# Two transformer blocks with split fp32 weights: the convolution with tokens on partitions, kr's first half from x without norm, two load queues and products of ones at first, and side jobs spread by traced durations

## The chip, the cores and the metric
One core of a Trainium2 chip. The metric is the device time of one execution in microseconds (us); one execution was profiled, and its trace is read here.

## The reference, cut to what matters
Two blocks run one after the other on 256 tokens of width 2048, batch 1, all fp32. Cut to what the change touches:

```
h = rms_norm(x) * norm_gain                    # block 1; u = h @ w_in, split into
q, k, v, z_a, f | r, kr, vr, z_b, w, a | g_a, g_b   # fox attention, rwkv7, two gates
u_rwkv = u + (u shifted by one token - u) * mu      # token shift of r, kr, vr, z_b, w, a
...
h = rms_norm(x) * norm_g_2                     # block 2; proj = h @ w_in_2, split into
cg, cb, cu, cz, c_q, c_kv, k_rope, mla_z, mem_q, mem_z, g_conv, g_mla, g_mem
conv_y = cb * causal_depthwise_conv(cg * cu, w)     # 3 taps along the tokens, 1024 channels
o_conv = (conv_y * silu(cz)) @ w_conv_out
o_mla, o_mem = latent attention of 16 heads, attention to 256 memory tokens
x = x + (sigmoid(g_conv)*o_conv + sigmoid(g_mla)*o_mla + sigmoid(g_mem)*o_mem) @ w_o
```

## The kernel before, in words
**Weights.** All weights lie in HBM as 659 blocks of 128x1024 fp32 (512 KB). SP loads a block into `raw` (`dma_to`, line 396), ACT rounds it to fp32r as `whi` (line 279), DVE subtracts the two as `wlo` (line 242). Four `raw` and four `whi`/`wlo` buffers exist. Activations are split in the same manner into a high and a low part. Each product of an activation with a weight is then three matmuls on PE: high by high, high by low, low by high, all from line 287.

**Two forms of gemm** (`gemm`, line 472). In the plain form the weights are the stationary operand, 256 columns (the tokens) stream, and each of four accumulators holds 128 channels by 256 tokens. In the form marked `tm` the activations are stationary, 512 weight columns stream, and each of two accumulators holds 128 tokens by 512 channels. There are five accumulator banks (`gpool`) and three banks for all else (`ppool`). The gates `ga`, `gb`, `gm`, `gc`, `gl`, the output projections and some others are `tm`; the convolution's four projections `cg`, `cu`, `cb`, `cz` are plain, twice each (`conv_groups(b)`, line 1494, for 512 channels at a time). After the last matmul of an accumulator, `evac` reads it on ACT or DVE; until then its bank is not free.

**The convolution before.** Channels are on partitions and tokens in the free direction, so a tap is a multiply by a column of parameters (`cw0` to `cw2`) with the source shifted by one or two columns. `cz` is gated and split at once into the pair `och`, `ocl`, which the gemm `co` takes later.

**Side jobs.** The recurrence of rwkv7, the attentions and the norms are generators (`spawn`). `pump()` (line 459), called between the matmuls of a gemm, steps them as long as an estimate of DVE's and ACT's time (`clock`) isn't too far ahead of an estimate of PE's. The costs in the estimate are constants: `CD` a DVE instruction, `CA` an ACT instruction, and a term in `mm` for a matmul. `finish(job)` steps a job to its end at once. A scheduler then fixes each engine's order from the order in which this recording wrote it; every engine runs its list in order, so an instruction that waits holds all that stands behind it. `hr` (in `head_rs`, line 597) is a per-head reciprocal root: DVE computes `hy` on a compact tile, a DMA of POOL writes it to HBM (`hd`), and two DMAs of POOL read it back in broadcast form.

**The start.** x comes in four tiles `xt`. Each is squared (ACT), reduced on DVE (`red`, to `r4`) and, after the last tile, summed over partitions by a product with ones, `ssq`; in the program's order the four `ssq` stand between the first gemms. Those gemms (the small `lora` ones and `r`) run from x times gain without the norm (`xg`), and the factor `rs` is applied at evacuation (`evac_scaled`, line 704); `kr` and `vr` follow from `h`, which `start_job` (line 752) makes. `par` (parameters) and `xt` are loaded by SP, interleaved with the first weights (lines 325, 388 to 396).

Of the kernel before, what the change touches and what calls it, by code (L numbers as in the profile page):

```python
# [26 lines left out]
def weight_groups():  # L27
# [4 lines left out]
    g = []  # L32
# [32 lines left out]
    def conv(b):  # L65
        for i, nm in enumerate(("cg", "cu", "cb", "cz")):
            add(f"{nm}{b}", w, 2048, _tiles((0, 2048, 1024, 3072)[i] + 512 * b, 4))

# [44 lines left out]
def pack_weights(inputs):  # L113
# [20 lines left out]
    ("fbias", 1), ("w0", 8), ("a0", 8), ("k_k", 8), ("k_a", 8), ("r_k", 8), ("ln_w", 8), ("ln_b", 8),  # L134
    ("fng", 16), ("ng2", 16), ("cw0", 8), ("cw1", 8), ("cw2", 8), ("qg", 4), ("kvg", 4),
    ("qn_g", 1), ("qr_g", 1), ("kn_g", 1), ("kr_g", 1), ("mem_g", 16), ("mqn_g", 2), ("mkn_g", 2),
# [9 lines left out]
def pack_params(inp):  # L146
    def flat(n):
        return np.asarray(inp[n]).reshape(-1)

    mix = flat("rwkv_shift_mix")  # L150
    zeros = np.zeros(128, np.float32)

    def padded(v):
        return np.concatenate([v, zeros[:128 - len(v)]])

    fb = np.zeros(128, np.float32)
    fb[96:104] = flat("fox_forget_bias")
    cw = np.asarray(inp["conv_w_2"]).reshape(3, 1024)
    v = {
        "norm_gain": flat("norm_gain"), "mu_r": mix[0:1024], "mu_kr": mix[1024:2048], "mu_vr": mix[2048:3072],  # L160
        "mu_zb": mix[3072:4096], "mu_wd": padded(mix[4096:4192]), "mu_ad": padded(mix[4192:4288]), "fbias": fb,
        "w0": flat("rwkv_w0"), "a0": flat("rwkv_a0"), "k_k": flat("rwkv_k_k"), "k_a": flat("rwkv_k_a"),
        "r_k": flat("rwkv_r_k"), "ln_w": flat("rwkv_ln_w"), "ln_b": flat("rwkv_ln_b"),
        "fng": flat("final_norm_gain"), "ng2": flat("norm_g_2"), "cw0": cw[0], "cw1": cw[1], "cw2": cw[2],
        "qg": flat("mla_q_norm_g_2"), "kvg": flat("mla_kv_norm_g_2"), "qn_g": flat("mla_qn_nope_g_2"),
        "qr_g": np.tile(flat("mla_qn_rope_g_2"), 2), "kn_g": flat("mla_kn_nope_g_2"),
        "kr_g": np.tile(flat("mla_kn_rope_g_2"), 2), "mem_g": flat("mem_norm_g_2"),
        "mqn_g": flat("mem_qn_g_2"), "mkn_g": flat("mem_kn_g_2"),
    }
# [58 lines left out]
def hybrid_kernel(ctx: ExitStack, tc: tile.TileContext, io, out):  # L228
# [95 lines left out]
    xt = [a4("xt") for _ in range(4)]  # L324
    nc.sync.dma_start(out=par, in_=io["params"])

# [53 lines left out]
    def dma_to(n):  # L380
        while st["dma"] < min(n, nblk):
            i = st["dma"]
            j = block_at(i)
            raw_t[j] = wpool.tile([128, 1024], F32, name=nm("raw"), tag="raw", bufs=NRAW)
            x = i // 3
            if i == 0:
                for p in range(2):
                    nc.sync.dma_start(out=xt[0][:, 2 * p:2 * p + 2, :], in_=io["xT"][:, 2 * p:2 * p + 2, :])
                    nc.sync.dma_start(out=raw_t[j][:, half(p)], in_=io["W"][j, :, half(p)])
            else:  # L390
                if i % 3 == 0 and x < 4:
# [239 lines left out]

    def sumsq_start(tiles, scales=None):

        ps = bank("ssq")
        n = len(tiles)
        for i, x in enumerate(tiles):
            sq = a4("sq")
            act(sq, x, AF.Square)
            r = b1("sqr")
            red(r, sq.rearrange("p a t -> p t a"), ALU.add)  # L640
            yield
            mm(ps[:, :256], ones, r, start=i == 0, stop=i == n - 1)
        sumsq_start.out = ps[:, :256]
# [772 lines left out]
    def latent_job(d, gain, name):  # L1416
# [74 lines left out]
    oc = []  # L1491
    cg = {}

    def conv_groups(b):
        gemm(f"cg{b}", h2, evac_copy(cg, b, "cg"))
        g, cv = cg.pop(b), out4("cv")

        def evac_u(c, ps):
            k = 4 * b + c
            u, v = g[:, c, :], cv[:, c, :]  # L1500
            mul(u, u, ps)
            ts(v, u, pc("cw2", k), ALU.mult)
            stt(v[:, 1:256], u[:, 0:255], pc("cw1", k), v[:, 1:256], ALU.mult, ALU.add)
            stt(v[:, 2:256], u[:, 0:254], pc("cw0", k), v[:, 2:256], ALU.mult, ALU.add)
        gemm(f"cu{b}", h2, evac_u)
        gemm(f"cb{b}", h2, lambda c, ps: mul(cv[:, c, :], cv[:, c, :], ps))
# [3 lines left out]
        def evac_cz(c, ps):  # L1510
            t = b1("cz")
            silu2(t, ps)
            stt(t, t, 0.5, cv[:, c, :], ALU.mult, ALU.mult)
            split(t, p[0][:, c, :], p[1][:, c, :])
# [258 lines left out]
```

## Time and profile before

| | |
|---|---|
| median of 3 runs | 2058.05 us (2056.01, 2058.05, 2065.45) |
| the profiled execution: its own time, its span | 2055.2 us, 2053.4 us |
| PE busy | 2021.0 us, 98% |
| DVE, ACT, POOL busy | 1304.9 us (64%), 968.3 us (47%), 73.9 us (4%) |
| HBM read | 365.76 MB, 181 GB/s over the span |

The profile's page gives busy times by engine, the chain of work that ended last (followed back from the last instruction), and the costliest groups. A matmul's record is longer than the distance to the next one, since they overlap; its price is therefore the distance between two starts. The granted clock is given for a stretch as a share of TensorE's full speed: 1.00 is 2.4 GHz, 0.50 is 1.2 GHz.

### The profile page before, as it was taken

To read this page: it belongs to the slowest core of one execution; us is meant where nothing else is said; L and a number is where in the kernel's file an instruction comes from. 1 tells how busy PE (TensorE), PEld (TensorE's weight loads), DVE (VectorE), ACT (ScalarE), POOL (GpSimd) and SP (SyncE) were. 2 spreads that over 40 slices of the span, in tenths; PEclk is the share of its full clock that TensorE was granted. 3 is DMA by queue.
4 is the path that set the end of the run, shared out by engine and by line. 5 is a ranking of instruction groups with operands and counts; after the bars stand their busy time and mean duration, and the time that the engine had idled before them with its cause. 6 is when DMAs were issued, how large, how long until landed. Compare 5 with 4: busy or idle time off the path is not lost.

```text
span 2053.4 us, 33342 instructions
## 1 busy us (share of the span) xinstructions
PE 2021.0 (98%) x13456; PEld 1822.4 (89%) x13456; DVE 1304.9 (64%) x1987; ACT 968.3 (47%) x1334; POOL 73.9 (4%) x133
## 2 busy tenths in 40 slices
PE   8999999998998999999999999999999999999999
PEld 8999989897777888898999999998888889988887
DVE  8776737868446478666865776755755655555554
ACT  6634435444444445554554435445545444444442
POOL 0002000020000000000000000000000000000000
PEclk9999999999999999999999999999999999999999
DMA  7555644544546656665555554556655555566564
GB/s 248 172 182 166 199 131 135 175 134 156 171 155 217 213 191 211 194 209 185 193 188 182 157 175 154 196 164 193 207 185 176 193 172 179 195 212 201 192 195 154
DMA packets 105674, 374.97 MB, mean 183 GB/s; under 512 B 12920, under 2 KB 13904, under 8 KB 105520
## 3 DMA queue, kind: packets, MB, share of 16 engines
q1 hardware_dynamic: 97568, 350.73, 52.8%
q0 software_dynamic: 7952, 22.12, 3.7%
q8 instruction: 105, 1.72, 0.3%
q14 instruction: 49, 0.40, 0.1%
HBM read 365.76 MB, written 5.86 MB: 181 GB/s over the span
## 4 chain that ended last, share of the span: by engine, by line
PE 94%; DMA 2%; DVE 2%; issue 1%; ACT 1%; POOL 0%; SPq 0%; DVEq 0%; ACTq 0%; POOLq 0%
PE acc.lz L287 4%; PE acc.ga L287 4%; PE acc.gb L287 4%; PE acc.gl L287 4%; PE acc.wo L287 4%; PE acc.w L287 4%; PE acc.lo L287 4%; PE acc.gc L287 4%; PE acc.gm L287 4%; PE acc.fq L287 2%; PE acc.r L287 2%; PE acc.zb L287 2%; PE acc.mz L287 2%; PE acc.mq L287 2%; PE acc.fk L287 2%; PE acc.mk L287 2%
## 5 line engine op out<-in xcount | busy, mean ns | idle before, releaser
L242 DVE TENSOR_TENSOR wlo<-raw,whi 128x1024 fp32r<-128x1024 f32 (+1 forms) x659 | 795.7, 1221 | 540.1 <-ACT whi L279 529.9
L279 ACT ACTIVATE whi<-raw 128x1024 fp32r<-128x1024 f32 (+1 forms) x659 | 683.1, 1055 | 757.3 <-issue 88.1
L287 PE MATMUL acc.lz<-h2h,whi 128*128 128x256 f32 x256 | 72.6, 284 | 0.0
L287 PE MATMUL acc.lz<-h2l,whi 128*128 128x256 f32 x256 | 72.6, 284 | 0.0
L287 PE MATMUL acc.lz<-h2h,wlo 128*128 128x256 f32 x256 | 72.5, 283 | 0.0
L287 PE MATMUL acc.gb<-wlo,hh 128*128 128x512 f32 x128 | 50.5, 398 | 6.0 <-DVE wlo L242 6.0
L287 PE MATMUL acc.ga<-whi,hh 128*128 128x512 f32 x128 | 50.9, 402 | 4.5 <-DVE zb L262 4.5
L287 PE MATMUL acc.ga<-whi,hl 128*128 128x512 f32 x128 | 51.2, 400 | 0.0
L287 PE MATMUL acc.ga<-wlo,hh 128*128 128x512 f32 x128 | 50.8, 397 | 0.0
L287 PE MATMUL acc.gb<-whi,hl 128*128 128x512 f32 x128 | 50.3, 397 | 0.0
L287 PE MATMUL acc.gl<-whi,h2h 128*128 128x512 f32 x128 | 50.0, 392 | 0.0
L287 PE MATMUL acc.gl<-wlo,h2h 128*128 128x512 f32 x128 | 50.0, 392 | 0.0
L287 PE MATMUL acc.gc<-whi,h2l 128*128 128x512 f32 x128 | 50.0, 392 | 0.0
L287 PE MATMUL acc.gl<-whi,h2l 128*128 128x512 f32 x128 | 50.0, 392 | 0.0
L287 PE MATMUL acc.w<-wlo,mgh 128*128 128x512 f32 x128 | 50.0, 390 | 0.0
L287 PE MATMUL acc.w<-whi,mgl 128*128 128x512 f32 x128 | 49.9, 390 | 0.0
L287 PE MATMUL acc.gm<-wlo,h2h 128*128 128x512 f32 x128 | 49.9, 391 | 0.0
L287 PE MATMUL acc.gc<-wlo,h2h 128*128 128x512 f32 x128 | 49.9, 391 | 0.0
L287 PE MATMUL acc.gm<-whi,h2l 128*128 128x512 f32 x128 | 49.8, 390 | 0.0
L287 PE MATMUL acc.gb<-whi,hh 128*128 128x512 f32 x128 | 49.6, 397 | 0.0
L287 PE MATMUL acc.wo<-whi,ml 128*128 128x512 f32 x128 | 49.5, 390 | 0.0
L287 PE MATMUL acc.wo<-wlo,mh 128*128 128x512 f32 x128 | 49.5, 389 | 0.0
(627 smaller groups left out, 6192.6 us busy)
## 6 DMA issues: line engine op xcount, KB each, us to landing
raw<-in_W SPq DMA_DIRECT2D x657, 512.0 KB, 4.0
hr<-hd POOLq DMA_DIRECT2D x10, 512.0 KB, 5.6
hr<-hd POOLq DMA_DIRECT2D x12, 256.0 KB, 5.5
xr<-in_xtm POOLq DMA_DIRECT2D x4, 512.0 KB, 6.6
mt<-in_memT POOLq DMA_DIRECT2D x4, 512.0 KB, 6.5
xbd<-x1g POOLq DMA_DIRECT2D x4, 512.0 KB, 3.0
xo<-xbd POOLq DMA_DIRECT2D x4, 512.0 KB, 5.3
out_tm<-xo SPq DMA_DIRECT2D x8, 256.0 KB, 4.2
```

Of the source, the lines that this page charges most:

```text
L242: DVE.tensor_tensor(out=o, in0=a, in1=b, op=op)
L279: ACT.activation(out=o, in_=a, func=f, scale=scale, **kw)
L287: TE.matmul(o, lhsT=l, rhs=r, start=start, stop=stop)
```

## The change
1. The convolution's four projections become `tm` (512 weight columns stream over stationary activations). Tokens are then on partitions, so a tap is no longer a shift of columns: `conv_job` copies u = cg*cu by DMAs of POOL to `ul`, one and two tokens (partitions) later, loads the taps broadcast to all partitions (`cw`, a new input `cwt`), and DVE multiplies and adds 512 columns at a time. `evac_cb` finishes that job before it reads cb's accumulator. The result is turned to channels on partitions by 16 transposes on PE (`make_pair`) before it is split.
2. At the start: `par` and the first x tile are issued by ACT's queue, the weights by SP's; five products of ones (`NWARM`) go to `ssq` before any data; the partial sums of squares are folded by adds on DVE (`fold`) and summed by one product of ones instead of four. The memory tokens' sum of squares and the two latent norms are folded likewise.
3. `kr`'s first half runs from `xg` with `rs` applied at evacuation; `start_job` is finished behind it, not ahead.
4. The constants of the estimates: `CD` 0.065 to 0.15, a matmul's cost 0.0133 + n/2400 us for n columns (at least 0.109), fp32 products n/600.

```diff
-            add(f"{nm}{b}", w, 2048, _tiles((0, 2048, 1024, 3072)[i] + 512 * b, 4))
+            add(f"{nm}{b}", w, 2048, _tiles((0, 2048, 1024, 3072)[i] + 512 * b, 4), tm=True)
...
-        clock["pe"] += max(0.000424 * n, 0.0001 + 0.0016 * fsz(l) / 2) if l.dtype == F32R else max(0.00168 * n, 0.00168 * fsz(l))
+        clock["pe"] += max(PEF + n / 2400.0, 0.109) if l.dtype == F32R else max(n / 600.0, fsz(l) / 1200.0)
...
-    nc.sync.dma_start(out=par, in_=io["params"])
+    nc.scalar.dma_start(out=par, in_=io["params"])
...
+    ssq = bank("ssq")[:, :256]
+    for _ in range(NWARM):
+        TE.matmul(ssq, lhsT=ones, rhs=one1.to_broadcast([128, 256]), start=True, stop=True)
...
-                    nc.sync.dma_start(out=xt[0][:, 2 * p:2 * p + 2, :], in_=io["xT"][:, 2 * p:2 * p + 2, :])
+                    nc.scalar.dma_start(out=xt[0][:, 2 * p:2 * p + 2, :], in_=io["xT"][:, 2 * p:2 * p + 2, :])
...
+    def fold(sq, r, i):
+
+        add(sq[:, 0:2, :], sq[:, 0:2, :], sq[:, 2:4, :])
+        if i:
+            add(r, r, sq[:, 0, :])
+            add(r, r, sq[:, 1, :])
+        else:
+            add(r, sq[:, 0, :], sq[:, 1, :])
...
-        red(r4[:, i, :], sq.rearrange("p a t -> p t a"), ALU.add)
+        fold(sq, r0, i)
...
-            for i in range(4):
-                mm(ssq, ones, r4[:, i, :], start=i == 0, stop=i == 3)
+            mm(ssq, ones, r0)
...
-    finish(j0)
-    xg.clear()
...
-    for key in ("kr", "vr"):
-        gemm(f"{key}0", h, evac_shift(key, 0))
+    gemm("kr0", xg, evac_scaled("kr", 0))
+    finish(j0)
+    xg.clear()
+    gemm("vr0", h, evac_shift("vr", 0))
...
+    def conv_job(b, u):
+
+
+        w = [tm4(a4("cw")) for _ in range(2)]
+        late = [tm4(a4("ul")) for _ in range(2)]
+        for i in range(2):
+            n = i + 1
+            POOL.memset(late[i][0:n, 0, :], 0.0)
+            POOL.dma_start(out=late[i][n:128, :, :], in_=u[0:128 - n, :, :])
+            POOL.dma_start(out=late[i][0:n, 1, :], in_=u[128 - n:128, 0, :])
+        POOL.dma_start(out=w[0], in_=io["cwt"][:, b, 0:2, :])
+        POOL.dma_start(out=w[1][:, 0, :], in_=io["cwt"][:, b, 2, :])
+        yield from lag()
+        wb = [w[1][:, 0, :], w[0][:, 1, :], w[0][:, 0, :]]
+        for t in range(2):
+            mul(u[:, t, :], u[:, t, :], wb[0])
+            yield
+            for i in range(2):
+                mul(late[i][:, t, :], late[i][:, t, :], wb[1 + i])
+                add(u[:, t, :], u[:, t, :], late[i][:, t, :])
+                yield
...
-        gemm(f"cg{b}", h2, evac_copy(cg, b, "cg"))
...
+        g = tm4(out4("cg"))
+        gemm(f"cg{b}", h2, lambda t, ps: acopy(g[:, t, :], ps))
+        gemm(f"cu{b}", h2, lambda t, ps: mul(g[:, t, :], g[:, t, :], ps))
+        jc = spawn(conv_job(b, g))
+
+        def evac_cb(t, ps):
+            finish(jc)
+            mul(g[:, t, :], g[:, t, :], ps)
+        gemm(f"cb{b}", h2, evac_cb)
...
+        def evac_cz(t, ps):
+            x = b2("cz")
+            act(x, ps, AF.Tanh, scale=0.5)
+            stt(x, x, 1.0, ps, ALU.add, ALU.mult)
+            stt(g[:, t, :], x, 0.5, g[:, t, :], ALU.mult, ALU.mult)
         gemm(f"cz{b}", h2, evac_cz)
+        make_pair(b, g, p)
...
+NWARM = 5
...
-CD, CA = 0.065, 0.17
+CD, CA, PEF = 0.15, 0.17, 0.0133
```

The new constants move instructions of the side jobs on DVE. Two places, both around a wait of PE. The first is where the second half of the recurrence's bonus (`CE`, `BV`) waits for its broadcast `hr`, between the last step of `hy`, from which that broadcast is made, and `CE`. DVE's list before:

```order
655 L242 TENSOR_TENSOR hy_6521<-hy_6521,ht_6522 128x256
656 L559 MEMSET mf_6581 128x1
657 L262 SCALAR_TENSOR_TENSOR mf_6581<-gate_6367,acc.pf_997_6596 128x512
658 L559 MEMSET gate_6665 128x1
659 L262 SCALAR_TENSOR_TENSOR mf_6581<-gate_6367,acc.pf_996_6595 128x512
660 L559 MEMSET mf_6815 128x1
661 L559 MEMSET gate_6893 128x1
662 L242 TENSOR_TENSOR obl_6916<-BV_1812,obh_6915 128x1024
663 L262 SCALAR_TENSOR_TENSOR mf_6815<-gate_6665,acc.pf_1038_6829 128x512
664 L262 SCALAR_TENSOR_TENSOR CE_6411<-CE_6411,par,hr_6537 128x256 x4
665 L262 SCALAR_TENSOR_TENSOR BV_4562<-CE_6411,par,BV_4562 128x256 x2
```

And DVE's list now:

```order
682 L241 TENSOR_TENSOR hy_6692<-hy_6692,ht_6693 128x256
683 L241 TENSOR_TENSOR wlo_7037<-raw_6966,whi_7036 128x1024
684 L561 MEMSET mf_6830 128x1
685 L261 SCALAR_TENSOR_TENSOR mf_6830<-gate_6638,acc.pf_1040_6845 128x512
686 L561 MEMSET gate_6908 128x1
687 L241 TENSOR_TENSOR wlo_7043<-raw_6972,whi_7042 128x1024
688 L261 SCALAR_TENSOR_TENSOR mf_6830<-gate_6638,acc.pf_1039_6844 128x512
689 L241 TENSOR_TENSOR obl_6931<-BV_1827,obh_6930 128x1024
690 L241 TENSOR_TENSOR wlo_7077<-raw_7004,whi_7076 128x1024
691 L261 SCALAR_TENSOR_TENSOR CE_6576<-CE_6576,par,hr_6738 128x256 x4
```

Three blocks of `wlo` stand between `hy` and `CE` where none stood.

The second is the evacuation of the first accumulator of `zb`'s second half, with the steps of the triangular solve (`TM`, `W`) ahead of it. The solve's steps widen from 64x31 to 64x256 and narrow again. DVE's list before (the steps at 64x220 and at 64x231 to 64x252 stand ahead of these rows):

```order
528 L242 TENSOR_TENSOR TM_5425<-W_752_5183,W_751_5182 64x255
529 L242 TENSOR_TENSOR W_752_5183<-W_752_5183,TM_5425 64x17x15
530 L242 TENSOR_TENSOR TM_5440<-W_752_5183,W_751_5182 64x256
531 L242 TENSOR_TENSOR W_752_5183<-W_752_5183,TM_5440 64x16x16
532 L242 TENSOR_TENSOR TM_5443<-W_752_5183,W_751_5182 64x255
533 L242 TENSOR_TENSOR W_752_5183<-W_752_5183,TM_5443 64x15x17
534 L262 SCALAR_TENSOR_TENSOR zb_5470<-acc.zb_762_5207,par,zb_5470 128x255
```

And DVE's list now (ahead of these rows another `wlo` and the steps up to the first at 64x135):

```order
525 L241 TENSOR_TENSOR wlo_5574<-raw_5370,whi_5573 128x1024
526 L241 TENSOR_TENSOR W_776_5350<-W_776_5350,TM_5429 64x27x5
527 L241 TENSOR_TENSOR TM_5432<-W_776_5350,W_775_5349 64x156
528 L241 TENSOR_TENSOR W_776_5350<-W_776_5350,TM_5432 64x26x6
529 L241 TENSOR_TENSOR TM_5447<-W_776_5350,W_775_5349 64x175
530 L241 TENSOR_TENSOR W_776_5350<-W_776_5350,TM_5447 64x25x7
531 L241 TENSOR_TENSOR TM_5450<-W_776_5350,W_775_5349 64x192
532 L561 MEMSET mf_6092 128x1
533 L241 TENSOR_TENSOR W_776_5350<-W_776_5350,TM_5450 64x24x8
534 L241 TENSOR_TENSOR TM_5453<-W_776_5350,W_775_5349 64x207
535 L241 TENSOR_TENSOR W_776_5350<-W_776_5350,TM_5453 64x23x9
536 L261 SCALAR_TENSOR_TENSOR zb_5480<-acc.zb_750_5154,par,zb_5480 128x255
```

The evacuation now stands after the steps up to 64x207, with two `wlo` among them (one is in these rows, the other just ahead); before, it stood after those up to 64x256 and the first past it.

## Rows read from the trace of the kernel before

**Rows 1.** The profile's page: busy time, share of the span and instructions by engine; then the chain that ended last, by engine.

```profile
PE 2021.0 (98%) x13456; PEld 1822.4 (89%) x13456; DVE 1304.9 (64%) x1987; ACT 968.3 (47%) x1334; POOL 73.9 (4%) x133
...
PE 94%; DMA 2%; DVE 2%; issue 1%; ACT 1%; POOL 0%; SPq 0%; DVEq 0%; ACTq 0%; POOLq 0%
```

**Rows 2.** What PE waited for: engine, waiting tile and line, the releaser, us in total, times, longest us.

```profile
PE lora L287 <- ACT xgh L279: 6.2, 1, 6.2
PE acc.gb L287 <- DVE wlo L242: 6.0, 1, 6.0
PE acc.ga L287 <- DVE zb L262: 4.5, 1, 4.5
PE acc.fz L287 <- DVE wlo L242: 2.3, 1, 2.3
...
PE ms L287 <- DVE mq L262: 1.2, 1, 1.2
PE mpt L1632 <- DVE msm L256: 1.0, 1, 1.0
```

**Rows 3.** The chain in order of time: start us, us, engine, tile, line, number of instructions. `cz` streams 256 columns, `lo` 512.

```profile
1213.35 17.04 PE acc.cz L287 x142
...
1805.71 21.76 PE acc.lo L287 x96
```

**Rows 4.** Timeline of PE, start us and us: six transposes in a row.

```profile
875.02 0.82 PE L530 MATMUL tr<-con,hx 128*128 128x128 f32 x6
```

**Rows 5.** Windows: us, busy of PE, PEld, DVE, ACT, POOL (with counts), the granted clock (PEclk), DMA share, GB/s. Rows of two such tables.

```profile
635.40:640.00 4.60, 4.59 (x11) 3.63 (x12) 4.60 (x9) 0.00 (x0) 0.56 (x1) 0.50 0.71 231
480.50:482.00 1.50, 1.49 (x4) 1.20 (x5) 0.85 (x2) 0.95 (x3) 0.00 (x0) 0.50 0.00 0
...
6.00:13.00 7.00, 6.81 (x27) 6.12 (x28) 6.72 (x9) 5.79 (x10) 0.00 (x0) 1.00 1.00 373
13.00:20.00 7.00, 7.00 (x59) 6.95 (x58) 6.92 (x12) 7.00 (x12) 0.00 (x0) 1.00 1.05 382
```

**Rows 6.** Timeline of DVE around the wait for `hr` at 632 us: start us, us, instruction, and in brackets the idle time before it and its releaser.

```profile
626.48 0.68 DVE L262 SCALAR_TENSOR_TENSOR mf<-gate,acc.pf 128x512 f32<-128x512 f32 x1
631.76 1.67 DVE L262 SCALAR_TENSOR_TENSOR CE<-CE,par,hr 128x256 f32<-128x256 f32 x4 [4.59 <-DMA hr<-hd]
...
634.14 1.22 DVE L242 TENSOR_TENSOR wlo<-raw,whi 128x1024 fp32r<-128x1024 f32 x1
```

**Rows 7.** Timeline of PE right behind that wait.

```profile
635.41 0.79 PE L287 MATMUL acc.gb<-wlo,hh 128*128 128x512 f32 x1 [5.98 <-DVE wlo L242]
...
636.42 0.63 PE L287 MATMUL acc.gb<-whi,hh 128*128 128x512 f32 x1
636.85 0.63 PE L287 MATMUL acc.gb<-wlo,hh 128*128 128x512 f32 x1
...
640.69 0.41 PE L287 MATMUL acc.gb<-wlo,hh 128*128 128x512 f32 x1
```

**Rows 8.** Timeline of DVE ahead of the evacuation of `zb`.

```profile
457.79 0.18 DVE L242 TENSOR_TENSOR TM<-W,W 64x31 f32<-64x31 f32 x1
...
479.65 0.42 DVE L242 TENSOR_TENSOR W<-W,TM 64x255 f32<-64x255 f32 x1
479.99 0.47 DVE L262 SCALAR_TENSOR_TENSOR zb<-acc.zb,par,zb 128x255 f32<-128x255 f32 x1
```

**Rows 9.** Timeline of PE in the first 20 us.

```profile
8.15 0.41 PE L287 MATMUL lora<-xgh,whi 128*128 128x256 f32 x1
8.36 0.41 PE L287 MATMUL lora<-xgl,whi 128*128 128x256 f32 x1
...
10.34 1.22 PE L287 MATMUL ssq<-sqr,one 128*128 128x256 f32 x2
...
11.57 0.41 PE L287 MATMUL acc.r<-xgl,whi 128*128 128x256 f32 x1
...
12.78 0.28 PE L287 MATMUL acc.r<-xgl,whi 128*128 128x256 f32 x1
12.90 0.28 PE L287 MATMUL lora<-xgh,wlo 128*128 128x256 f32 x1
...
19.12 0.59 PE L287 MATMUL ssq<-sqr,one 128*128 128x256 f32 x2
...
19.67 0.28 PE L287 MATMUL lora<-xgh,whi 128*128 128x256 f32 x1
```

**Rows 10.** Timeline of the start on DVE, SP's queue and ACT.

```profile
0.81 0.06 DVE L342 MEMSET one<- 128x1 f32 x1 [0.81 <-PEq L1765]
...
1.65 0.42 SPq L389 DMA_DIRECT2D raw<-in_W  x1
...
5.10 0.63 ACT L279 ACTIVATE whi<-raw 128x512 fp32r<-128x512 f32 x1 [3.09 <-DMA raw<-in_W]
```

**Rows 11.** Groups of DVE's instructions by line and form: line, engine, operation, tiles, shapes, number | busy us, mean ns of one | idle before it. The second and third rows are of the stretch 1190 to 1290 us.

```profile
L270 DVE TENSOR_REDUCE sqr<-sq 128x256 f32<-128x1024 f32 x8 | 16.1, 2031 | 0.3 <-ACT sq L279 0.3
...
L242 DVE TENSOR_TENSOR cv<-cv,acc.cb 128x256 f32<-128x256 f32 x4 | 1.7, 415 | 0.0
...
L242 DVE TENSOR_TENSOR oml<-mof,omh 128x512 fp32r<-128x512 f32 x2 | 1.4, 686 | 0.0
```

**Rows 12.** The page's DMA issues: tiles, queue, number, KB each, median us from issue to landing.

```profile
hr<-hd POOLq DMA_DIRECT2D x10, 512.0 KB, 5.6
```

More of the change, by code (lines that the diff above doesn't have):

```diff
@@ L134 @@
     ("fbias", 1), ("w0", 8), ("a0", 8), ("k_k", 8), ("k_a", 8), ("r_k", 8), ("ln_w", 8), ("ln_b", 8),
-    ("fng", 16), ("ng2", 16), ("cw0", 8), ("cw1", 8), ("cw2", 8), ("qg", 4), ("kvg", 4),
+    ("fng", 16), ("ng2", 16), ("qg", 4), ("kvg", 4),
     ("qn_g", 1), ("qr_g", 1), ("kn_g", 1), ("kr_g", 1), ("mem_g", 16), ("mqn_g", 2), ("mkn_g", 2),
@@ L157, in pack_params @@
     fb[96:104] = flat("fox_forget_bias")
-    cw = np.asarray(inp["conv_w_2"]).reshape(3, 1024)
     v = {
@@ L163, in pack_params @@
         "r_k": flat("rwkv_r_k"), "ln_w": flat("rwkv_ln_w"), "ln_b": flat("rwkv_ln_b"),
-        "fng": flat("final_norm_gain"), "ng2": flat("norm_g_2"), "cw0": cw[0], "cw1": cw[1], "cw2": cw[2],
+        "fng": flat("final_norm_gain"), "ng2": flat("norm_g_2"),
         "qg": flat("mla_q_norm_g_2"), "kvg": flat("mla_kv_norm_g_2"), "qn_g": flat("mla_qn_nope_g_2"),
@@ L630, in hybrid_kernel, with sumsq_start @@
     dma_to(NRAW)
-    def sumsq_start(tiles, scales=None):
+    def fold(sq, r, i):
[5 more added lines that the diff above has]
+            add(r, sq[:, 0, :], sq[:, 1, :])
+    def sumsq_start(tiles):
         ps = bank("ssq")
-        n = len(tiles)
+        r = b1("sqr")
         for i, x in enumerate(tiles):
@@ L638, in sumsq_start @@
             act(sq, x, AF.Square)
-            r = b1("sqr")
-            red(r, sq.rearrange("p a t -> p t a"), ALU.add)
+            fold(sq, r, i)
             yield
-            mm(ps[:, :256], ones, r, start=i == 0, stop=i == n - 1)
+        mm(ps[:, :256], ones, r)
         sumsq_start.out = ps[:, :256]
@@ L663, in hybrid_kernel @@
     xg = []
-    r4 = a4("sqr")
+    r0 = b1("sqr")
     def start_tile(i):
@@ L711, in evac_scaled @@
         return f
-    ssq = bank("ssq")[:, :256]
     acc_l = [bank("lora")[:, :256] for _ in range(2)]
@@ L749, in hybrid_kernel @@
                 del hi_t[j], lo_t[j]
-    del ssq, r4
+    del ssq, r0
     def start_job():
@@ L1421, in latent_job @@
         r = b1("lr")
-        red(r, sq.rearrange("p a t -> p t a"), ALU.add)
+        fold(sq, r, 0)
         yield
@@ L1491, in hybrid_kernel @@
     oc = []
-    cg = {}
-    def conv_groups(b):
-        gemm(f"cg{b}", h2, evac_copy(cg, b, "cg"))
[L1496 to L1506, printed above, removed]
+    def conv_job(b, u):
[17 more added lines that the diff above has]
+                yield
+    def conv_groups(b):
+        g = tm4(out4("cg"))
[6 more added lines that the diff above has]
+        gemm(f"cb{b}", h2, evac_cb)
         p = out_pair("oc")
         oc.append(p)
[L1510 to L1514, printed above, removed]
+        def evac_cz(t, ps):
[3 more added lines that the diff above has]
+            stt(g[:, t, :], x, 0.5, g[:, t, :], ALU.mult, ALU.mult)
         gemm(f"cz{b}", h2, evac_cz)
+        make_pair(b, g, p)
     lo = {}
@@ L1755 @@
         "fng": np.ascontiguousarray(np.broadcast_to(a["final_norm_gain"].reshape(1, 2048), (128, 2048))),
+        "cwt": np.ascontiguousarray(np.broadcast_to(
+            a["conv_w_2"].reshape(3, 2, 512).transpose(1, 0, 2)[None], (128, 2, 3, 512))),
         "memT": channel_major(a["mem_2"]),
```

## The prediction
> **What bounds the kernel now.** Read the page first: PE is busy 98% of the span, and the chain that ended last is PE for 94% of it [rows 1]. So the time is what PE issues, priced by the distance between two starts, plus the few places where PE stands still. The list of what PE waited for names those: 6.2 us for the first data, 6.0 us at `acc.gb`, 4.5 us at `acc.ga`, 2.3 us at `acc.fz`, about 1 us each at `ms` and `mpt` [rows 2]. DVE at 64% and ACT at 47% matter only where their list in order makes one of these waits, and DMA only at the start. The sum is made against the profiled execution, 2055.2 us; it lies 2.9 us below the median of the three runs. Half a per cent, some 10 us, is about what a measurement of this kernel can tell from no change.
>
> **Wider streams in the convolution.** The eight gemms issue 1536 matmuls of 256 columns and would issue 768 of 512. A run of `cz` takes 17.04/142 = 0.120 us a matmul, a run of `lo`, which has the new form, 21.76/96 = 0.2267 us [rows 3]. 768 x (0.240 - 0.2267) = **-10.2 us**, all of it on PE and so on the path. The new form loads a stationary tile for each matmul as `lo` does, so nothing is left to find out here.
>
> **Transposes.** 16 more on PE. Six in a row take 0.82 us with a record of 0.27 each [rows 4], so (0.82 - 0.27)/5 = 0.11 us from one to the next: **+1.8 us**. The bounds are 0 (they fill a gap) and the whole record, 16 x 0.27 = 4.3. I take the spacing, because here too they come in fours between matmuls. The Trainium skill, TensorE: Matmul & The Clock Gate, section "Part 4: PE-mode transpose", speaks against this part: it gives about 275 ns for a transpose in a kernel. This trace's record agrees with that length but not with that price, as the next one starts 0.11 us later; by the page's figure the term would be 4.4 us and the forecast 2.6 us higher, an estimate.
>
> **The wait at `gb`.** DVE's list reaches `CE` after `mf` at 626.48, idles 4.59 us for the broadcast `hr`, and only behind `CE` and `BV` makes the next `wlo`, at 634.14 [rows 6]; PE waits 5.98 us [rows 7]. There is more: after it, starts are 0.43 us apart and the granted clock is 0.50, the level of 1.2 GHz [rows 5, 7], until 640.69. From 636.42 to 640.69 are ten distances, with the one before it eleven, that cost 0.2 us each more than 0.2267: 2.2 us. With 0.4 us in the first distance the place costs 6.0 + 0.4 + 2.2 = 8.6 us. In the new list three `wlo`, two `mf` and `obl` stand between `hy` and `CE`. At 1.15 us a `wlo` they keep DVE at work during most of that wait and give PE three blocks, each worth 12 matmuls, 12 x 0.2267 = 2.7 us. The `wlo` behind `CE` still comes about 11 us after `hy`; PE then has 8 us of blocks beside what it holds. I leave 0.8 us: **-7.8 us** (0 to -8.6; nothing if DVE waits as long with PE already out of blocks).
>
> **The wait at `ga`.** With four banks held by `zb`, the second accumulator of `ga` needs `zb`'s first evacuation, which stood behind solve steps of 0.42 us until 479.99 [rows 8]. 4.5 us of wait [rows 2], 0.4 in the first distance, six at 1.2 GHz (granted clock 0.50 [rows 5]) for 1.2 us, and 1.3 us in small waits just ahead, all on the same run of DVE: 7.4 us. In the new list the evacuation stands behind the steps from 64x31 to 64x207, whose distances run from about 0.2 to 0.4 us: some 5.6 us, plus two `wlo` of 1.2 and the evacuation, about 9 us, and these begin 2 us before `zb` ends on PE. PE brings 24 matmuls of `ga` (5.4 us) and six small ones before it needs the bank. So about 7 against 6 us, a wait of 1 us, too short to cost the clock: **-6.2 us** (0 to -7.4).
>
> **The start.** The first `lora` product starts at 6.19, and until 12.78 distances are 0.21 us for 256 columns where 12.78 to 12.90 is 0.12 [rows 9]; that is the 1.2 GHz level by the distance, though the granted clock reads 1.00 there [rows 5]. Some 24 matmuls at it cost 2.3 us. The five new products of ones come before all data. One costs 0.55 - 0.12 = 0.43 us at the high level (19.12 to 19.67 with one `lora` inside) and at the low one 1.23 - 0.21 = 1.02 at most (10.34 to 11.57 with one `acc.r` inside) [rows 9]: five are 2.2 to 5.1 us. Their operand is set at 0.81 [rows 10], so they end by 6.0 and hide behind the wait for data. Three products of ones fewer are 1.3 us, the slow first one 0.6 more. The first `raw` is issued at 1.65 in SP's queue and ACT waits for it until 5.10 [rows 10]; put first in that queue it goes out 0.9 us earlier. All of it would be 2.3 + 1.9 + 0.9 = 5.1 us. But DVE is busy 6.72 of 7 us and then 6.92 of 7, with the DMA share at 1.00 and 373 GB/s [rows 5], so PE can't run far ahead of what arrives. `fold` relieves DVE a little: the reduction of 2.03 us becomes an add of 0.69 and two of 0.41, 1.5 us [rows 11]. I take **-2.5 us**, half-way (-0.5 to -5.1). Taking `kr` from `xg` adds four multiplies of 0.4 us on DVE and takes the wait for `h` out of the way of a start that is earlier by that much; `h` is needed 192 x 0.12 = 23 us later, which covers it.
>
> **Small terms.** The memory tokens' sum needs three products of ones fewer: -1.3 us at 0.43. The waits at `ms` and `mpt` are 2.2 us [rows 2], and the memory attention is packed otherwise: -1 (0 to -2.2). The other waits keep their place. POOL gets 12 DMA issues and some 3.5 MB; it is busy 4% [rows 1], and this hides unless a rival below is right.
>
> **New waits in the convolution.** DVE's work is about what it was: a half has 20 operations of 0.69 us [rows 11], 13.7 us, against 32 short ones. But `finish` and two long multiplies per evacuation bunch them: `qn` needs four of five banks while `cz` still holds two. The trace doesn't show this; the nearest rows bound it by nothing and by the 8.6 us that a bunch of DVE work cost at `gb`. I take **+2 us**, the size of the small DVE waits in [rows 2].
>
> **Sum.** -10.2 + 1.8 - 7.8 - 6.2 - 2.5 - 1.3 - 1 + 2 = -25.2; 2055.2 - 25.2 = **2030 us**.
>
> **Rivals.** *The waits move, not go.* DVE's order changes everywhere, and a late `wlo` or evacuation can appear at another place; for it speaks that each of the big waits came from a bunch in that order, against it that the costs in the estimate now spread them. Width, transposes and ones products remain (-9.7), and 1 us at the start: 2044. Chance 0.22. *All gains come whole*: both waits to zero (-1.8 more), the start at -5.1 (-2.6), nothing new in the convolution (-2), and half of `fz` with its slow clock (-2): 2022. Chance 0.13. *The start doesn't do what it says*: warm products end late or the clock is low again when data come, DMA-bound all the same: 2055.2 - 22.7 = 2033 without the start's gain, 2038 if the five products (5.1 us) delay the first data; counted in the forecast's own range. *Slower*: `evac_cb` waits in DVE's list for the shifted copies `ul`, and all `wlo` stand behind it. Issue to landing of the 512 KB broadcasts on the same queue is 5.6 us [rows 12]; six such transfers are by that at most some 10 us from `cu`'s end, and DVE's ten operations 7 more, against 96 x 0.2267 = 21.8 us of `cb`. To end slower by 10 us over the median the copies must cost PE 13 + 25 = 38 us, 19 per half, so they would have to land about 34 us after `cu`, three times my estimate: then 2068 or more. The page SBUF — State Buffer of the Trainium skill, section "SBUF: two separate sides", has such a mechanism: a DMA issued from POOL can be held while DVE runs certain operations. No row here shows it at that size; the wait for `hr` lasted 4.59 us with DVE idle [rows 6]. Chance 0.03.
>
> **How the numbers follow.** Forecast 0.62 (2023 to 2038), moved waits 0.22, whole gains 0.13, slower 0.03. The range 2019 to 2046 takes in the second and third with the unknown ends. Faster by over 0.5% means under 2047.8: the forecast, the whole gains, and nearly all of the moved waits, 0.88; within 0.5% 0.09; slower 0.03.
>
> **What would show it.** `cg` to `cz` at 0.227 us per 512 columns; no wait over 2 us at `gb` and `ga`, and no stretch at granted clock 0.50 behind them; the first `lora` by 6 us with 0.12 us distances within some 2 us. Wrong it is if PE shows a new wait over 3 us between `cg` and `gm` or behind a moved block of DVE's list, or if `kr` starts no earlier.

## The result and the profile after

The changed kernel takes 2048.05 us (median of five runs, 2042.8 to 2050.19) against 2059.69 for the kernel before (five runs, 2056.01 to 2065.45): ratio 0.9934, interval 0.9909 to 0.9958, which is 12 us less by the medians and some 14 by the ratio. The forecast was 2030 in a range of 2019 to 2046. The profiled execution took 2044.08 us, its span 2042.3, 11.1 us less than before.

The page: PE issues as forecast (768 matmuls fewer in the convolution, 16 transposes, 10 records of the five products of ones, 12 records fewer of the sums: 12702 for 13456) and is busy 99% [rows 1].

```profile
PE 2013.4 (99%) x12702; PEld 1781.0 (87%) x12702; DVE 1301.7 (64%) x1982; ACT 969.0 (47%) x1322; POOL 82.4 (4%) x149
```

What PE waited for, columns as in [rows 2]:

```profile
PE acc.fz L286 <- DVE wlo L241: 4.2, 1, 4.2
PE mpt L1659 <- DVE msm L255: 3.6, 2, 2.2
PE acc.mo L286 <- DVE wlo L241: 2.9, 1, 2.9
PE u L286 <- DMA XA<-Xd: 1.9, 2, 1.4
PE acc.cu L286 <- DVE wlo L241: 1.8, 2, 1.7
PE acc.fv L286 <- DVE wlo L241: 1.4, 1, 1.4
PE acc.cz L286 <- DVE wlo L241: 1.3, 2, 1.0
PE lora L286 <- ACT xgh L278: 1.3, 1, 1.3
...
PE acc.gb L286 <- DVE wlo L241: 1.0, 1, 1.0
...
PE acc.ga L286 <- DVE zb L261: 0.5, 1, 0.5
```

The two waits that the forecast took away are gone: `gb` 6.0 to 1.0, `ga` 4.5 to 0.5. In their place stand one at `fz` that has grown from 2.3 to 4.2, several that the list of before didn't have (`cu`, `fv`, `cz`), one at `mo` that was 0.5, and a longer `mpt`. Without the first 20 us, `ga` and `gb`, PE's waits were 11.2 us in sum and are 20.5.

The convolution's matmuls and the transposes, from the chain and the timeline of PE; they answer to [rows 3, 4]. From one start to the next it is 2.27/10 = 0.227 us for a matmul and, with a record of 0.27, (0.60 - 0.27)/3 = 0.11 us for a transpose:

```profile
1342.78 2.27 PE acc.cz L286 x10
```

```profile
1247.74 0.60 PE L532 MATMUL tr<-con,cg 128*128 128x128 f32 x4
```

The start on PE, which answers to [rows 9]:

```profile
0.93 4.08 PE L345 MATMUL ssq<-one 128*128 128x256 f32 x10 [0.93 <-DVE one L341]
6.27 0.50 PE L286 MATMUL lora<-xgh,whi 128*128 128x256 f32 x2 [1.26 <-ACT xgh L278]
...
7.33 0.28 PE L286 MATMUL lora<-xgh,whi 128*128 128x256 f32 x1
7.45 0.28 PE L286 MATMUL lora<-xgl,whi 128*128 128x256 f32 x1
```

The five products end at 5.0. The first `lora` comes no earlier than before (6.27 for 6.19), but from 7.33 on the distances are 0.12 us, where before they were 0.21 until 12.78. That is so in this execution; below, most others with the new start differ. `kr` starts at 42.91 where it started at 45.81.

So where did the gain go? The start of some gemms, read from both timelines (us):

| first matmul of | before | after | difference |
|---|---|---|---|
| `kr`, first half | 45.8 | 42.9 | -2.9 |
| `fz`, first half | 249.9 | 245.9 | -4.0 |
| `ga` | 466.0 | 470.5 | +4.5 |
| `pr` | 724.6 | 713.0 | -11.6 |
| `krope` | 1001.3 | 988.3 | -13.0 |
| `qr`, second quarter of the heads | 1398.5 | 1384.4 | -14.1 |
| `gc` | 1526.2 | 1517.1 | -9.1 |
| end of PE | 2049.1 | 2038.0 | -11.1 |

8.5 us are lost between 250 and 470, the convolution's region (1001 to 1398) gives 1 us where 6 were forecast (with `ms` and `mpt` 7), and 5 are lost behind it. Of the 8.5 us, 3.9 are more idle time of PE (8.6 for 4.7); the mean granted clock there is 0.977 for 0.992, and 12 small matmuls (`fs`, `fo`) now stand ahead of `ga` that stood behind it. What DVE waited for points to the cause; first before, then after (only the waits that a DMA ended):

```profile
DVE qr L262 <- DMA hr<-hd: 10.7, 2, 8.0
DVE kn L262 <- DMA hr<-hd: 10.3, 3, 5.9
...
DVE qn L262 <- DMA hr<-hd: 9.3, 4, 4.7
DVE KK L242 <- DMA hr<-hd: 8.7, 2, 6.7
...
DVE rot L242 <- DMA rot<-qr: 5.6, 2, 5.0
```

```profile
DVE qn L261 <- DMA hr<-hd: 15.2, 4, 7.5
DVE kn L261 <- DMA hr<-hd: 13.4, 4, 6.2
DVE KK L241 <- DMA hr<-hd: 11.4, 2, 8.9
DVE qr L261 <- DMA hr<-hd: 10.9, 2, 8.2
DVE rot L241 <- DMA rot<-qr: 10.4, 2, 7.5
...
DVE ul L241 <- DMA cw<-in_cwt: 4.0, 1, 4.0
```

DVE's list stands at round trips: `hr`, which goes over HBM, and `rot`, a copy of `qr` to other partitions by four DMAs of POOL. Every `wlo` behind such a wait is held until it ends. The timeline of DVE and PE at `mo` shows one whole: DVE makes two blocks, stands 7.54 us for `rot`, and PE runs out of blocks, then runs on at the level of 1.2 GHz (0.43 us a distance; the granted clock of 1434.4 to 1437.3 is 0.52).

```profile
1420.88 2.35 DVE L241 TENSOR_TENSOR wlo<-raw,whi 128x1024 fp32r<-128x1024 f32 x2
1430.77 1.22 DVE L241 TENSOR_TENSOR rot<-rot,sin 128x1024 f32<-128x1024 f32 x1 [7.54 <-DMA rot<-qr]
1431.91 1.22 DVE L241 TENSOR_TENSOR qr<-qr,cos 128x1024 f32<-128x1024 f32 x1
1433.05 2.35 DVE L241 TENSOR_TENSOR wlo<-raw,whi 128x1024 fp32r<-128x1024 f32 x2
```

```profile
1434.32 0.67 PE L286 MATMUL acc.mo<-wlo,omh 128*128 128x512 f32 x1 [2.90 <-DVE wlo L241]
1434.78 0.63 PE L286 MATMUL acc.mo<-whi,oml 128*128 128x512 f32 x1
1435.21 0.63 PE L286 MATMUL acc.mo<-whi,omh 128*128 128x512 f32 x1
```

The same place before, in the same order, had DVE wait 5.03 us and PE 0.5: only the DMA took less time.

```profile
1441.45 1.23 DVE L242 TENSOR_TENSOR rot<-rot,sin 128x1024 f32<-128x1024 f32 x1 [5.03 <-DMA rot<-qr]
```

At `fz` it is likewise. The two blocks behind `hy` and the operations behind `KK`, the first use of `hr`, are those of before; what differs is how long DVE stood for `hr`, before and after:

```profile
388.39 1.23 DVE L242 TENSOR_TENSOR KK<-KK,hr 128x1024 f32<-128x1024 f32 x1 [6.67 <-DMA hr<-hd]
```

```profile
390.40 1.23 DVE L241 TENSOR_TENSOR KK<-KK,hr 128x1024 f32<-128x1024 f32 x1 [8.93 <-DMA hr<-hd]
```

### The profile page after: what moved, and what is told of

Read it like the earlier page. It is cut to its first block, busy times and chain, and to the rows that moved or that the text cites. A ratio compares the mean times of both kernels' runs of the same rounds, so it can differ in the third digit from the quotient of the medians.

```text
span 2042.3 us, 31847 instructions
## 1 busy us (share of the span) xinstructions
PE 2013.4 (99%) x12702; PEld 1781.0 (87%) x12702; DVE 1301.7 (64%) x1982; ACT 969.0 (47%) x1322; POOL 82.4 (4%) x149
## 5 line engine op out<-in xcount | busy, mean ns | idle before, releaser
L286 PE MATMUL acc.w<-whi,mgh 128*128 128x512 f32 x128 | 49.5, 391 | 0.0
L286 PE MATMUL acc.gm<-whi,h2h 128*128 128x512 f32 x128 | 49.5, 390 | 0.0
## 6 DMA issues: line engine op xcount, KB each, us to landing
hr<-hd POOLq DMA_DIRECT2D x12, 256.0 KB, 7.1
out_tm<-xo SPq DMA_DIRECT2D x8, 256.0 KB, 4.2
```

## The experiments

Medians; ratios are to runs of the kernel before on the same chip. From the first `lo` to the end of PE every profile here takes 243.4 or 243.5 us, so the chips don't differ in speed and times may be compared across them. The sums of DVE's idle time that DMAs ended count places over 1 us behind 100 us: 54.9 us in the kernel before, 81.2 in the changed one.

**Each part alone.** e1 takes the whole of `conv_groups` and `tm=True` into the kernel before, e2 the constants:

```diff
-CD, CA = 0.065, 0.17
+CD, CA, PEF = 0.15, 0.17, 0.0133
```

with the new term in `mm`; e5 the changed kernel's start with the old convolution and the old constants. "Theory A" to "Theory E" are the rival accounts that the expectations name.

> The kernel before with the convolution's new form alone (tokens on partitions, shifted copies, transposes); start, kr and constants as before. Theory A (the waits that ate the gain come from the new constants' order on DVE): the 1100 to 1390 us region keeps the waits of before and gains 10.2 - 1.8, so 8 us less than before, about 2047 in a profiled run of 2055. Theory B (the form itself brings them: fewer points at which side jobs are stepped, DVE's list standing at hr with less work ahead of it, copies in POOL's queue beside hr): DVE idles 25 us or more for hr and rot between 1100 and 1240 (15.9 before, 31.4 after), and the region gains 0 to 3 us, about 2053.

> The kernel before with the new cost constants alone. Both theories: the waits at ga and gb fall to under 1.5 us each (-14 us). Theory A: new waits of 8 us between 250 and 480 and of 8 us around the convolution and acc.mo, net 0 to +3, about 2055. Theory B: only those between 250 and 480 come, the convolution's region stays as before, net -6, about 2049.

> The kernel before with the new start alone (two load queues, products of ones at first, folded sums, kr's first half from x); convolution and constants as before. Theory C (the start's gain is real and lasts): kr starts 3 us earlier, 1.3 us from the memory tokens' sum, so 4 us less than before, 2051 in a profiled run. Theory D (behind the start, DVE's list around hr is ordered otherwise and the gain is given back by 400 us): 0 to +4 us, with a wait at acc.fz of over 3 us where 2.3 stood.

Measured: e1 2060.98 us, ratio 1.000 (0.9982 to 1.0019); e2 2039.43, 0.9911 (0.9881 to 0.9942); e5 2061.84, 1.0001 (0.9986 to 1.0016). The constants alone give more than the whole change; the wider convolution and the start give nothing alone. In e1 the profile shows what stands against the 10 us that PE issues less: PE's own idle time is 33.2 us for 27.8 (3.3 of these 5.4 us lie ahead of 450 us, where the convolution has not begun), and DVE's idle time at DMAs is 77.1 us (23.8 of it between 1100 and 1240, where 15.9 stood).

```profile
DVE kn L262 <- DMA hr<-hd: 24.1, 4, 8.9
DVE qn L262 <- DMA hr<-hd: 15.0, 4, 6.4
...
DVE rot L242 <- DMA rot<-qr: 8.8, 2, 6.5
```

That is theory B in kind, a little under its number; theory A's 8 us less did not come. In e5 the total is theory D's, but not at its place: PE waits 2.4 us at `zb` and 2.2 at `fv`, not at `fz`. In e2 DVE's idle time at DMAs is 55.4 us, and the waits of PE are few:

```profile
PE lora L287 <- ACT xgh L279: 6.2, 1, 6.2
PE ms L287 <- DVE mq L262: 3.6, 1, 3.6
PE acc.fv L287 <- DVE wlo L242: 1.7, 1, 1.7
PE u L287 <- DMA XA<-Xd: 1.3, 1, 1.3
```

My expectation of e2 was too high under both theories: no new wait came at `fz`. Its timeline there shows two blocks of `wlo` right behind the first use of `hr`; in the changed kernel, as in the kernel before, six other operations stand between (`KK` at 390.40, first `wlo` at 394.22).

```profile
383.11 1.22 DVE L242 TENSOR_TENSOR KK<-KK,hr 128x1024 f32<-128x1024 f32 x1 [6.30 <-DMA hr<-hd]
384.25 2.35 DVE L242 TENSOR_TENSOR wlo<-raw,whi 128x1024 fp32r<-128x1024 f32 x2
```

**Each part undone.** e3 is the changed kernel with the old convolution, e6 with the old constants, e7 with the old start (the edits of above, backwards).

> The changed kernel with the convolution in its old form (256 columns stream, taps as parameter columns). Theory A: the waits stay and the width is lost, +8 us over the changed kernel, 2052 against its profiled 2044. Theory B: the region from 1100 to 1390 takes what it took in either kernel, within 2 us of the changed kernel.

> The changed kernel with the old cost constants. If the constants alone carry the gain (as before with the new constants, 2035.7 profiled, says), the waits at gb and ga come back and the run is that of before or 3 us less, 2050 to 2055. If the parts add, it is 4 + 0 less than before, also about 2051; over 2058 would mean that the other two parts cost time by themselves.

> The kernel before with the new convolution and the new constants, the old start. Theory D (the new start costs some 8 us between 250 and 480 us under the new constants): no wait over 1.5 us at acc.fz, 2036 to 2040. Theory E (the convolution costs it): 2043 or more, with the loss between 1100 and 1240 us.

Measured: e3 2041.41 (0.9921, 0.9896 to 0.9946), less than the changed kernel's 2048; e6 2059.77 (0.9985, 0.9970 to 0.9999); e7 2044.49 (0.9917, 0.9884 to 0.9950). Under the new constants, putting in the convolution takes 2041.4 to 2048.1, putting in the start 2044.5 to 2048.1: neither pays, and the intervals overlap. Theory A fails at e1, e2 and e3. Theory D fails at e7 by its time: the wait at `fz` is gone, but one of 4.2 us stands at `cz` and one of 3.2 at `mo`. That is theory E's number (2043 or more), though its longest wait, `cz` at 1331, lies behind the place that theory E named. e6 is over its 2058, but so was the kernel before beside it (2061): the other two parts cost nothing by themselves, and gain next to nothing. Its waits are back, 6.2 us at `gb` and 4.5 at `ga`. The wait moves about; no part owns it.

**Later in the recording.**

```diff
-LAG, HOP = 5, 0.0
+LAG, HOP = 10, 0.0
```

> The changed kernel with LAG 10 for 5: a side job that waits for a round trip over HBM is taken up again 10 us of estimated PE time later, for traced round trips of 10 to 12 us. If DVE standing in its list at hr, rot and cw is what makes PE wait (fz, mpt, mo, cu, cz, some 20 us with the low clock behind them), DVE's idle time ended by those DMAs falls from 68 us to under 25 and the run is 8 to 14 us shorter than the changed kernel, about 2033. Rival: the waits are due to bunches of DVE work, not to DMAs; then DVE's idle time falls but the run stays within 3 us of the changed kernel.

Measured: 2039.96 (0.991, 0.9875 to 0.9944), 8 us less than the changed kernel by the medians, with intervals that overlap. DVE's idle time at DMAs is 81.3 us, as in the changed kernel: if there is a gain, it is not by the reason given, and what made it is open. Counted in DVE's lists, the blocks of `wlo` between the last step of `hy` and the first use of `hr` are 42 over 16 round trips in the kernel before, 43 in the changed one, 43 here. The scheduler puts the use 2 or 3 blocks behind as a rule (0 to 4), and doubling `LAG` did not change that; the trace's trip takes longer (`hd` issued at 376.49, `KK` free to go at 390.40).

**Without the round trip.** `hr` is loaded from a weight block ahead of its job. `hy` is computed and written out, but nothing reads it, so the normalisation is left out. The broadcast DMAs fall away, and the scheduler orders DVE's list anew.

```diff
+        out = a4("hr")
+        POOL.dma_start(out=out, in_=io["W"][0].rearrange("p (a b) -> p a b", a=4))
         ps = bank("hs")[:, :256]
...
-            POOL.dma_start(out=out, in_=d[0:4, :].unsqueeze(0).to_broadcast([128, 4, 256]))
...
-            for e in range(2):
-                POOL.dma_start(out=out[64 * e:64 * e + 64, :, :], in_=d[e:8:2, :].unsqueeze(0).to_broadcast([64, 4, 256]))
```

e8 does it to the changed kernel, e13 to the kernel before, e9 to e11 to the changed kernel with one part undone.

> The changed kernel with hr loaded from a weight block in HBM ahead of its job's work, not from hy over HBM: hy is still computed and written out, but nobody waits for it. It leaves out the heads' normalisation, so its output is not the reference's. If DVE standing in its list at hr is what makes PE wait at fz, mpt, cu, cz, ms and gb, DVE's idle time ended by hr goes from some 55 us to under 5, these waits go, the one at mo (behind rot, which stays) remains, and the run is 10 to 16 us shorter than the changed kernel, 2029 to 2034 profiled. If bunches of DVE work make them, it stays within 4 us.

> The kernel without the round trip of e8 (hr not the reference's), with the convolution in its old form. If the form is worth what the sum said and only the round trips hid it, it is 10.2 - 1.8 - 1 to 3 of small waits, 5 to 8 us longer than e8: 2019 to 2022. If its own copies and bunches eat it, within 2 us of e8.

> The kernel without the round trip of e8 (hr not the reference's), with the old cost constants. If the constants act on two things, DVE's wait for hr at gb and the solve steps ahead of zb's evacuation at ga, then the wait at gb stays away and the one at ga is back: 6 to 8 us longer than e8, about 2020. If they act through hr alone, within 2 us of e8.

> The kernel without the round trip of e8 (hr not the reference's), with the old start. If the start is worth its terms (2.5 and 1.3 us) it is 3 to 5 us longer than e8, 2017 to 2018; if it gives nothing, within 1.5 us.

> The kernel before without the round trip (hr from a weight block, not the reference's). With e8 to e11 the three parts are worth 7.3, 4.1 and 6.1 us where no round trip stands in DVE's list; if they add, this is 2013.7 + 17.5 = 2031. Then the round trips cost the kernel before 27 to 30 us and the changed kernel 34, and the difference is where the forecast went. If it is below 2026, the parts overlap and the round trips cost the kernel before as much as the changed one.

| without the round trip | us | ratio to the kernel before | against e8 |
|---|---|---|---|
| e8, the changed kernel | 2013.71 | 0.9767 (0.9744 to 0.9790) | |
| e9, old convolution | 2021.05 | 0.9817 (0.9801 to 0.9832) | +7.3 |
| e10, old constants | 2017.81 | 0.9805 (0.9788 to 0.9823) | +4.1 |
| e11, old start | 2019.79 | 0.9811 (0.9796 to 0.9827) | +6.1 |
| e13, the kernel before | 2029.53 | 0.9860 (0.9842 to 0.9877) | +15.8 |

PE's waits in e8 (over 0.15 us) are these:

```profile
PE lora L286 <- ACT xgh L278: 1.1, 1, 1.1
PE u L286 <- DMA XA<-Xd: 1.1, 1, 1.1
PE ssq L345 <- DVE one L341: 0.9, 1, 0.9
```

Not one `wlo` is late. e8 went 16 us or more beyond what I expected: the wait at `mo` went too, since DVE no longer stood for `rot`, though its DMAs were left as they were. Here the convolution and the start are worth about what the sum gave them, and the three parts add (17.5 against 15.8). The round trips of `hr` cost the kernel before 30 us and the changed one 34. e10 missed: the wait at `ga` did not come back (0.7 us, as in e13), so it too had hung on `hr`, probably by the solve that starts behind `KK`. Of the constants' 20 us in e2 some 16 are thus, by an estimate that sets e2 against e10, a better place of the waits for `hr`.

**The taps' loads apart from hr.**

```diff
+        w = [tm4(a4("cw")) for _ in range(2)]
+        POOL.dma_start(out=w[0], in_=io["cwt"][:, b, 0:2, :])
+        POOL.dma_start(out=w[1][:, 0, :], in_=io["cwt"][:, b, 2, :])
         gemm(f"cg{b}", h2, lambda t, ps: acopy(g[:, t, :], ps))
```

> The changed kernel with the taps' broadcast loads (cw, 0.75 MB per half) issued ahead of cg's gemm and not in one burst behind hr and beside the shifted copies. If the burst delays hr (7.2 and 7.6 us to landing beside it, 5.0 and 4.0 in the kernel before) and DVE (idle 4.0 us for cw), hr lands 1 to 2 us sooner there and the wait for cw goes: 2 to 5 us less than the changed kernel. If not, within 2 us.

Measured: 2044.24 (0.9924, 0.9903 to 0.9945) against 0.9934: not told apart. The wait for `cw` went (one of 3.2 us for `ul` took its place), but `hr` lands no sooner: 7.0 and 8.4 us at the two places where it took 7.2 and 7.6, and a median of 7.0 where the changed kernel has 5.5:

```profile
hr<-hd POOLq DMA_DIRECT2D x10, 512.0 KB, 7.0
```

The burst of `cw` is not what delays it. The shifted copies were left where they were.

**The wait held behind more blocks.** The DMAs are the same; the place of the wait in DVE's list is moved, by a tie to a later `wlo` (0 times it is added to one element), and the job is taken up later in the recording (18 or 22 us of estimated PE time for 5).

```diff
+    def behind(cell):
+        if lo_t:
+            lo = lo_t[max(lo_t)]
+            stt(cell, lo[64:65, 0:1].bitcast(F32), 0.0, cell, ALU.mult, ALU.add)
...
-        yield from lag()
+        yield from lag(HLAG)
+        behind(out[64:65, 0, 0:1])
```

and so for `rot`. e14 (`HLAG` 18) and e15 let a job read another one's `hr` in places; e16 and e17 (`HLAG` 18 and 22) set `head_rs.out` behind the hold, so that each reads its own.

> The changed kernel with the wait for hr and rot held behind later blocks: one element of hr gets 0 times an element of the newest wlo added, 18 us of estimated PE time behind the issue, so that DVE's list has the wlo up to that block ahead of the wait (72 blocks over 16 round trips, 43 in the changed kernel). If the place of the wait in DVE's list is the cause, DVE's idle time ended by DMAs falls from 84 us to under 45, and the run is 10 to 20 us shorter than the changed kernel, 2025 to 2035. If contention of the DMAs is, the idle time moves and the run stays within 4 us.

> The kernel before with the new constants and the same hold behind later blocks (80 blocks over 16 round trips). By the same reason 8 to 15 us less than the constants alone, 2024 to 2031; by the rival within 4 us of 2039.

> e14 with each job reading its own hr (in e14 and e15 a job could read that of another one, since the longer hold let two jobs overlap). If the place of the wait is the cause, as e14's 17 us say, this is also 10 us or more below the changed kernel, 2025 to 2037, with DVE's idle time ended by DMAs under 55 us.

> As e16 with the hold at 22 us instead of 18 (80 blocks over 16 round trips instead of 72). If more blocks ahead of the wait help further, 2 to 5 us less than e16; if the waits left are elsewhere (wlo at gb, u, the first data), within 3 us of e16.

Measured: e14 2030.7 (0.9861, 0.9840 to 0.9883), e15 2036.88 (0.9897, 0.9878 to 0.9917), e16 2026.9 (0.9853, 0.9832 to 0.9873), **e17 2023.71 (0.9827, 0.9809 to 0.9844)**: 34 us less than the kernel before, 24 less than the changed one. 72, 80, 72 and 80 blocks now stand between `hy` and the first use of `hr`, and DVE's idle time at DMAs is 41.0, 23.8, 39.7 and 36.2 us. So moving the wait gives back 24 of the 34 us that the trips cost the changed kernel, with the trips still made. No run has the longer hold without the tie; e4, with a hold of 10 and no tie, left both the blocks and the idle time as they were. e17 and e16 are not told apart. e15 gained only 2.6 over the constants alone, less than I expected, though its idle time fell most; the short list of waits above suggests that little was left to gain there. DVE's idle time is thus no price by itself: e2 has the sum of the kernel before (55.4 and 54.9 us) and takes 20 us less. What counts is whether PE runs out of blocks meanwhile. Of PE's waits in e17 one is long; DVE stands 6.35 us for `hr` just ahead of it, at 705.45:

```profile
PE acc.pr L286 <- DVE wlo L241: 7.9, 1, 7.9
PE lora L286 <- ACT xgh L278: 1.5, 1, 1.5
```

## Why the prediction was wrong

The step that failed is the one on small terms, "The other waits keep their place", with the +2 us for new waits in the convolution: the sum gave all waits other than those at `gb`, `ga` and the first data +1 us (-1 and +2), and they grew by 9.3 us (11.2 to 20.5). What they hang on is DVE's waits for the round trips, which had no term in the sum: without the trips of `hr` these waits of PE are gone, but for 1.1 us at `u`, and the changed kernel takes 34 us less (e8). The other terms first.

*Width and transposes*: right in price (0.227 and 0.11 us) and, where DVE waits for no `hr`, nearly in worth: 7.3 us in e9 for -10.2 + 1.8 = -8.4, or -6.4 with the +2. With the trips in place they gave nothing that could be measured (e1, e3).

*The wait at `gb`*: right in cause and, with luck, in size; 1.0 us left, with no stretch at the low clock. The trip took 14.0 us there where it had taken 7.6, DVE idled 5.3 us for it all the same, and the `wlo` behind `CE` was ready 17 us after `hy`, not 11; PE had more work in hand than the three blocks counted. *The wait at `ga`*: right in size (0.5 left for 1 forecast; 7.4 less that 1 is 6.4 and not 6.2, which changes nothing). The cause was only half right: shorter steps ahead of the evacuation were read from the list, and with the old constants the wait is back (4.5 us in e6), but e10 shows the wait gone under the old constants too once `hr` is not waited for.

*The start*: -2.9 us at `kr` and -4.0 at 250 us for -2.5. The low clock is gone as said in the profile of the changed kernel, in e6 and in e14. In the other nine profiles with the new start 11 to 18 of the first distances are 0.21 again, here in e8:

```profile
7.99 0.41 PE L286 MATMUL lora<-xgh,whi 128*128 128x256 f32 x1
8.20 0.41 PE L286 MATMUL lora<-xgl,whi 128*128 128x256 f32 x1
```

So the products of ones don't keep the clock up in every execution, and the gain hangs little on it: `kr` starts at 42.9 to 43.9 in all twelve, at 45.7 to 47.8 in the seven with the old start. The first product of data came no earlier: ACT's first rounding starts 1.0 us sooner (4.10 for 5.10), but a second one, which waits 0.46 us for its data, now stands ahead of `xgh`, and that starts at 5.72 for 5.64. With the memory tokens' term it is 6.1 us in e11 for 3.8; 1.9 of these are a wait at `bon` that e11 has and e8 has not.

*Small terms* failed: the other waits did not keep their place. I had compared DVE's order around each wait and found the same number of blocks there; but at `fz` and `mo` the same order gave longer waits (4.2 for 2.3 and 2.9 for 0.5), since the trip itself took another time (`rot`: 7.54 us of idle time for 5.03; `hr` at `KK`: 8.93 for 6.67), and the list around `mpt`, `cu` and `cz` was new. Nor is a wait near 1 us always too short to cost the clock, as I had it at `ga`: behind waits of 1.4 and 0.5 us at `u` PE ran at the 1.2 GHz level from 257.0 to 260.4 (granted clock 0.51), and in e8 behind one of 1.1 from 256.0 to 259.4 (0.51), where waits of 1.0 and 0.6 had left it at 1.00 before.

*New waits in the convolution* at +2 was the second: the region lost its 7 us gain. The mechanism named there, a bunch of long operations at the evacuation, wasn't the one; DVE stood at `hr`, and the new form raises DVE's idle time at DMAs by itself: between 1000 and 1400 us it is 16 to 22 us in the four profiles with the old form (before, e2, e3, e5) and 34 to 46 in the six with the new one and no hold (e1, e4, e6, e7, e12 and the changed kernel). The +9.3 us of waits and the slow clock behind `u`, `fz` and `mo` (outside `ga` and `gb` PE ran 11.7 us at the low level where it had run 3.4; at half speed that is some 4 us lost, an estimate) make most of the 14 us between 2030 and 2044.

The rival *the waits move, not go* is what happened, at its price, 2044; I gave it 0.22. What stood against it, that the new costs spread them, holds for bunches of work, not for a DMA's time: in the estimate that stands in `LAG` alone, 5 us against trips of 7.6 to 14 us, and e4 shows that `LAG` doesn't set the place of the wait. The slower rival (copies `ul` landing 34 us late) was far off: they took 8 to 10 us.

Why the new form makes DVE stand longer at `hr` the traces answer in part. Over the six trips between 1100 and 1390 us, the time from the last step of `hy` to the first use of `hr` is 62.0 us before and 64.3 in e1, with 16 blocks of `wlo` in either. But DVE has 5.0 us of other work on the way where it had 9.8, and 7.8 us of other waits where it had 17.4. So DVE gets to the wait sooner, rather than `hr` later. Why the time of one and the same trip varies stays open; e12 rules out the burst of `cw` as the reason, but not the shifted copies.

## What to carry to other kernels

Where an engine with idle time makes the operands of the engine that bounds, list its in-order waits for DMAs first: what a change saves elsewhere can be lost again at any of them. Price an edit once with those waits taken away (other data, nothing waited for), where it shows its own worth, and then fix the place of the wait; here a tie to a later block, with a longer hold, moved it where a hold of 10 us alone did not.

## What the runs showed of the hardware

Four runs each of the programs without the trips of `hr` (e8, e9, e10, e11, e13) lie within 1.8 to 4.6 us; four runs each of e2, e4, e7 and e12, with the trips, within 6.7 to 11.8, and 14 of the kernel before within 13.6. With the trips but the wait held behind more blocks (e14 to e17) it is 2.9 to 7.0. So most of the scatter comes with the waits for the trips.

The same four DMAs of `rot` ahead of `mo`, issued by POOL in 2.0 us in either profile, took 2.3 to 5.0 us to landing before and 2.3 to 7.5 after; the 256 KB DMAs of `hr` (halves) had a median of 5.5 us, then 7.1:

```profile
hr<-hd POOLq DMA_DIRECT2D x12, 256.0 KB, 7.1
```

A wait of 4.2 us at `fz` left PE at the 1.2 GHz level for 20 matmuls (granted clock 0.50, 0.21 us from one to the next for 0.12), 1.9 us more. Behind two waits at `u`, 1.4 and 0.5 us, the granted clock was 0.51 for 19 matmuls. The stretches at `u` and at `fz`, columns as in [rows 5]:

```profile
257.00:260.40 3.40, 3.40 (x19) 3.40 (x17) 0.00 (x0) 0.93 (x2) 0.00 (x0) 0.51 0.36 140
395.50:399.90 4.40, 4.40 (x20) 4.40 (x21) 4.39 (x5) 0.38 (x1) 0.00 (x0) 0.50 0.63 207
```
